# Alternating long and short head pairs in a transformer layer, and two weight scans moved to earlier pairs

## The chip, the cores and the metric

The kernel runs on one core of a Trainium2 chip. Its time is that of one execution on the device, in microseconds, taken as the median of several runs; less is better. TensorE (PE) does the matmuls, VectorE (DVE) and ScalarE (ACT) the elementwise work, GpSimd (POOL) some of it too, and SyncE (SP) issues most of the DMAs, the transposes among them. Each engine works through its own list of instructions in order and waits on semaphores for the others.

## The reference

One layer (DEPTH is 1) over 2048 positions of width 1024, in float32. The part that the change touches is the attention:

```python
h = rmsnorm(x, attn_norm_g[l])
proj = h @ w_in[l]
qa, ka, va, qb, kb, vb = jnp.split(proj, 6, axis=-1)
oa = chunked_band_attention(...)   # 8 heads, each query chunk of 64 sees 9 key chunks
ob = diff_attention(...)           # 4 heads of two maps each, every earlier key is seen
x = x + jnp.concatenate([oa, ob], axis=-1) @ w_out[l]
h = rmsnorm(x, ffn_norm_g[l])
u = causal_dwconv(h @ w_up[l], conv_w[l], conv_b[l])
gate, val = jnp.split(u, 2, axis=-1)
x = x + (jax.nn.silu(gate) * val) @ w_down[l]
```

The 8 band heads make four head pairs, numbered 0 to 3. The 4 differential heads, each of two maps, make four more, numbered 4 to 7.

## The kernel before

All products are made in float16 with each operand split into a high and a low part, three matmuls for one. First the normalised input is made and transposed (`make_h`), and the first pair's keys, values and some queries are projected. Then `attention()` goes through the eight head pairs in the order of the list `ORDER`, 16 row tiles of 128 queries each. Pairs 0 to 3 have **short rows**: a row tile sees at most 640 keys. Pairs 4 to 7 have **long rows**: row tile i sees (i + 1) x 128 keys, up to 2048, and the tiles are taken in the order 0, 15, 1, 14 and so on, so that a long tile follows a short one.

A step is one row tile. Its front (`front_a` for short rows, `front_b` for long ones) makes the scores on TensorE (L434), adds the bias and takes the maximum on VectorE into an `St` buffer (L478 and L537), takes the exponential on ScalarE (L486 and L544), splits the result into high and low halves (`phl`, on ScalarE, VectorE and GpSimd) and transposes it by DMA from SP (`pt<-phl`, L489 and L565). Its back (`back_a`, `back_b`) multiplies by the values (L509, L583), two steps later (`LAG`). Between the fronts and backs stand portions of projection work (`units`, L375): the remaining queries of this pair, and keys, values and first queries of the next one. A pair has 48 portions, the last but one 32 and the last 28 (`CHUNKS`). A portion is 6 matmuls of 512 columns for keys and values, or 12 of 256 columns for queries.

`beside(n)` lists what else is put into which step of the n-th pair (n counts from 0, by place in `ORDER`): the loading and scaling of the next pairs' weights (`scan_w`, `load_w`), and at the end three pieces of preparation for what comes after. `scan_wo` loads the eight row blocks of `w_out`, 512 KB each, through the two `wraw` buffers, and squares and sums each on ScalarE (L606) into `wam`. `scan_wd` loads two row blocks of `w_down` and takes their maxima on VectorE (L614, then `wd_factor`); its result is first used in the feed-forward stage. `load_wo` in the last pair uses `wam`, loads `w_out` a second time and makes its two halves. The output projection (`out_proj`) begins in the last pair's last steps; after it come the feed-forward stages.

The instructions' order on each engine is decided when the program is built: fronts and backs are issued with high priority, so a scheduler lets them pass the portions and the pieces of `beside`.

## Time and profile before

| | us |
|---|---|
| median of 3 runs | 2524.24 |
| lowest, highest | 2523.07, 2527.94 |
| the profiled execution's own time | 2528.28 |
| its span, first to last instruction | 2526.5 |
| attention, first pair's first factor to last pair's last | 81.0 to 1103.8 |
| mean granted TensorE clock | 0.975 |

| engine | busy us | share |
|---|---|---|
| TensorE (matmul) | 2379.4 | 94% |
| VectorE | 1846.0 | 73% |
| ScalarE | 1354.3 | 54% |
| GpSimd | 1164.6 | 46% |

The busy time of an engine is the union of its instructions. A matmul's end is modelled in the profile, and at a lower granted clock the same matmul counts as busy for longer. The granted clock is given as a share of 2.4 GHz: 1.00 is that, 0.50 is 1.2 GHz, and a value between them is a mean over the stretch.

### The profile page before, as it was taken

The page shows a single profiled execution, that of the slowest core. Times are in us where ns is not written, and L with a number is a line of the kernel's source. Part 1 is how long each engine was busy: PE and PEld are TensorE (multiplying, and loading weights), DVE is VectorE, ACT ScalarE, POOL GpSimd, SP SyncE. Part 2 cuts the span into 40 slices and gives each one's busy share as a digit, 9 for nine tenths or more (in the row PEclk, how much of TensorE's full clock was granted, in tenths as well). Part 3 has the DMA queues.
Part 4 walks back from the last instruction along what each step waited for, and adds up shares of the span by engine and source line. Part 5 has one row for each costly group of instructions (what it writes and reads, how often), then busy time and mean ns, then how long its engine had stood idle before and what let it go on. Part 6 is the DMA issues. An engine that isn't in the chain of part 4 may idle for free.

```text
span 2526.5 us, 42303 instructions
## 1 busy us (share of the span) xinstructions
PE 2379.4 (94%) x15382; PEld 1219.7 (48%) x15382; DVE 1846.0 (73%) x4359; ACT 1354.3 (54%) x2399; POOL 1164.6 (46%) x1127
## 2 busy tenths in 40 slices
PE   6999899999899988997978999999999999999998
PEld 5655555555565555543433444444444444444443
DVE  8678787568757885766566888888888776656555
ACT  7566566456655666644335666566556553333322
POOL 3343443234323332224234665666566464766654
PEclk9999899999999999998999999999999999999999
DMA  6154457635673579895995324333333339323322
GB/s 192 29 101 88 94 104 139 121 73 96 134 143 73 100 128 226 162 242 167 277 225 154 123 96 129 106 121 97 123 112 111 105 111 398 101 88 113 109 88 80
DMA packets 625378, 333.34 MB, mean 132 GB/s; under 512 B 447864, under 2 KB 592528, under 8 KB 623760
## 3 DMA queue, kind: packets, MB, share of 16 engines
q1 hardware_dynamic: 615264, 316.15, 50.2%
q0 software_dynamic: 2432, 8.42, 0.9%
q10 hardware_dynamic: 7472, 6.06, 0.8%
q8 instruction: 120, 1.97, 0.3%
q14 instruction: 90, 0.74, 0.1%
HBM read 145.73 MB, written 82.08 MB: 90 GB/s over the span
## 4 chain that ended last, share of the span: by engine, by line
PE 36%; DVE 6%; DMA 3%; ACT 3%; issue 2%; POOL 2%; SPq 1%; ACTq 0%; DVEq 0%; POOLq 0%
PE mm L859 21%; PE mm L1258 13%; DMA wd<-gd 2%; DVE Y L1058 1%; SPq L1093 1%; PE omm L654 1%; DVE wdhl L889 1%; ACT wuraw L959 1%; DMA T<-td 1%; DMA wdraw<-in_w_down_dram 0%; DMA wd<-wdd 0%; ACT Y L1062 0%; ACT wdhl L886 0%; DVE hl L681 0%; POOL wuhl L977 0%
## 5 line engine op out<-in xcount | busy, mean ns | idle before, releaser
L859 PE MATMUL mm<-T,wuhl 128*128 128x512 f16 x3696 | 809.0, 381 | 18.2 <-ACT tmp L1030 14.9
L859 PEld LDWEIGHTS <-wuhl 128*128 128x128 f16 x3696 | 363.4, 99 | 456.2 <-issue 25.5
L1258 PE MATMUL mm<-wd,ghl 128*128 128x512 f16 x1848 | 401.9, 380 | 4.7 <-ACT ghl L133 3.5
L375 PEld LDWEIGHTS <-whl 128*128 128x128 f16 x2976 | 273.1, 99 | 233.6 <-issue 81.4
L375 PE MATMUL mm<-h,whl 128*128 128x512 f16 x1440 | 349.2, 385 | 0.0
L434 PE MATMUL s<-ks,qs 64*128 64x256 f16 (+3 forms) x2160 | 282.1, 295 | 29.0 <-DVE mx L478 14.4
L1258 PEld LDWEIGHTS <-ghl 128*128 128x128 f16 x1848 | 180.7, 98 | 225.2 <-ACT ghl L133 4.8
L563 POOL TENSOR_TENSOR phl<-St,phl 128x1024 f16<-128x1024 f32 (+7 forms) x96 | 155.7, 1633 | 248.8 <-ACT phl L562 233.7
L1058 DVE SCALAR_TENSOR_TENSOR Y<-U,taps,Y 128x1024 f32<-128x1024 f32 x176 | 256.9, 1460 | 6.2 <-ACT Y L1054 4.6
L544 ACT ACTIVATE St<-St,nb,sc 128x1024 f32<-128x1024 f32 (+4 forms) x192 | 187.9, 979 | 50.3 <-DVE nb L541 50.3
L133 ACT ACTIVATE ghl<-wd,gsc 128x384 f16<-128x384 f32 (+1 forms) x176 | 106.6, 660 | 196.6 <-DMA wd<-gd 92.1
L134 DVE SCALAR_TENSOR_TENSOR ghl<-wd,gsc,ghl 128x384 f16<-128x384 f32 (+1 forms) x176 | 137.0, 812 | 94.3 <-ACT ghl L133 94.0
L375 PE MATMUL mq<-h,whl 128*128 128x256 f16 x1536 | 205.0, 278 | 0.0
L488 POOL TENSOR_TENSOR phl<-St,phl 128x640 f16<-128x640 f32 (+2 forms) x64 | 80.9, 1264 | 255.0 <-ACT phl L487 246.3
L434 PEld LDWEIGHTS <-qs 64*128 64x128 f16 x2160 | 114.4, 96 | 152.5 <-issue 108.0
L537 DVE CUSTOM_DVE_ANT_0 St<-s,near,mxb 128x512 f32<-128x512 f32 (+2 forms) x280 | 166.7, 620 | 25.5 <-PE s L434 19.8
L654 PE MATMUL omm<-wohl,oT 128*128 128x512 f16 x672 | 155.6, 386 | 18.5 <-DVE x L660 18.5
L889 DVE SCALAR_TENSOR_TENSOR wdhl<-wdraw,wd_sc,wdhl 128x128 f16<-128x128 f32 x132 | 141.5, 1087 | 30.8 <-ACT wdhl L886 29.7
L968 POOL TENSOR_TENSOR Sx<-wuraw 128x512 f32<-128x512 f32 x44 | 77.4, 1760 | 163.2 <-ACT wuraw L959 156.0
L1062 ACT ACTIVATE Y<-Y 128x1024 f32<-128x1024 f32 x44 | 46.5, 1057 | 182.2 <-DVE Y L1058 182.2
L486 ACT ACTIVATE St<-St,nb,sc 128x640 f32<-128x640 f32 (+4 forms) x128 | 107.9, 843 | 59.3 <-DVE nb L483 58.1
L562 ACT ACTIVATE phl<-St 128x1024 f16<-128x1024 f32 (+7 forms) x96 | 75.6, 802 | 114.1 <-DMA pt<-phl 56.6
(229 smaller groups left out, 3765.9 us busy)
## 6 DMA issues: line engine op xcount, KB each, us to landing
wd<-gd SPq DMA_DIRECT2D x88, 256.0 KB, 2.8
wuraw<-in_w_up_dram SPq DMA_DIRECT2D x42, 512.0 KB, 5.2
gd<-Y SPq DMA_DIRECT2D x42, 512.0 KB, 2.8
wdraw<-in_w_down_dram SPq DMA_DIRECT2D x154, 128.0 KB, 2.8
wd<-wdd SPq DMA_DIRECT2D x11, 1792.0 KB, 13.1
wdd<-wdhl SPq DMA_DIRECT2D x41, 448.0 KB, 2.7
wraw<-in_w_in_dram SPq DMA_DIRECT2D x24, 512.0 KB, 3.9
td<-hl SPq DMA_DIRECT2D x24, 512.0 KB, 5.0
```

What stands on the lines that cost most here:

```text
L134: V.scalar_tensor_tensor(lo, src, scale, hi, ALU.mult, ALU.subtract)
L375: nc.tensor.matmul(ps, lhsT=hl[:, a, c, :], rhs=h[:, b, c, t0:t1], start=n == 0, stop=n == 3 * NC - 1)
L434: nc.tensor.matmul(ps[hd], lhsT=qs[a:b, qa, qc], rhs=ks[a:b, ka, kc], start=n == 0, stop=n == 2)
L486: A.activation(St, St, AF.Exp, bias=nb[:, hd:hd + 1], scale=w["sc"], accum_out=l[:, hd:hd + 1])
L537: V.tensor_tensor_reduce(Sm[hd][g][:, a0:a0 + b - a], ps[hd][:, :b - a], bias, 1.0, m[hd], ALU.add, ALU.max, mx[:, hd, f:f + 1])
L544: A.activation(Sm[hd][g], Sm[hd][g], AF.Exp, bias=nb[:, hd:hd + 1], scale=w["sc"], accum_out=l[:, hd, g:g + 1])
L563: nc.gpsimd.tensor_tensor(hl[:, 1], Sm[0][g], hl[:, 0], ALU.subtract)
L654: nc.tensor.matmul(ps[n], lhsT=oc[:, a], rhs=wo[ORDER[c]][:, b, n * TG:(n + 1) * TG], start=k == 0, stop=k == 3 * NC - 1)
L859: nc.tensor.matmul(ps, lhsT=hl[:, a, wop, c * P:(c + 1) * P], rhs=Tt[:, b, c, :], start=start and k == 0, stop=k == 11, skip_group_check=n ...
L889: V.scalar_tensor_tensor(dst, src, scale, h, ALU.mult, ALU.subtract)
L1058: V.scalar_tensor_tensor(Y, self.U[j][:, tap:D + tap], self.u.taps[j][:, tap:tap + 1], Y, ALU.mult, ALU.add)
L1258: nc.tensor.matmul(ps[m].rearrange("p (c n) -> p c n", c=4), lhsT=g[kb][:, a, go], rhs=wd[kb][:, :, c_, wo_], start=kb == k0 and k == 0, s ...
```

## The change

The list `ORDER` is changed so that long and short rows alternate: 4, 0, 5, 1, 6, 2, 7, 3. The first and the last pair stay what they were. `scan_wo` moves from step 10 of the last but one pair to step 10 of the third pair, and `scan_wd` from step 13 of the last but one pair to step 10 of the fifth. The numbers of portions still go by place: the last but one pair, now the long pair 7, has 32.

```diff
-        ORDER = [4, 5, 0, 6, 1, 7, 2, 3]
+        ORDER = [4, 0, 5, 1, 6, 2, 7, 3]
...
-            if n == NH2 - 2:
+            if n == 2:
                 todo[10, 0] = scan_wo
-                todo[13, 0] = scan_wd
+            if n == 4:
+                todo[10, 0] = scan_wd
             if n == NH2 - 1:
                 todo[8, 1] = load_wo
```

The first place is SP's list at the passage from the first pair to the second. `pt<-phl` at L565 is the transpose of a long row tile's probabilities, at L489 of a short one's (the middle number of the shape is the count of 128 x 128 blocks), `ost<-ohl` and `oTd<-ost` carry the pair's output away. Before:

```order
L565 DMA_TRANSPOSE pt<-phl 128x2x128 x2
L447 DMA_TRANSPOSE ost<-ohl 128x8x128
L451 DMA oTd<-ost 256x1x512
L565 DMA_TRANSPOSE pt<-phl 128x16x128 x2
L447 DMA_TRANSPOSE ost<-ohl 128x8x128
L565 DMA_TRANSPOSE pt<-phl 128x4x128
```

Now:

```order
L565 DMA_TRANSPOSE pt<-phl 128x2x128
L489 DMA_TRANSPOSE pt<-phl 128x4x128
L447 DMA_TRANSPOSE ost<-ohl 128x8x128
L489 DMA_TRANSPOSE pt<-phl 128x8x128
L451 DMA oTd<-ost 256x1x512
L489 DMA_TRANSPOSE pt<-phl 128x12x128
L489 DMA_TRANSPOSE pt<-phl 128x16x128
```

The last long tile of the first pair was followed by the second pair's longest tile at once; now short tiles follow it.

The second place is ScalarE's list around the squares of `w_out` (L606, `woraw` is a row block). L486 and L544 are the exponentials of short and long rows, L487 and L562 the copies to the high half, L588 the squares of a long pair's output, L133 the high halves of projected keys, values and queries. Before, in the seventh pair:

```order
L486 ACTIVATE St,l<-St,nb,sc 128x640 x2
L606 ACTIVATE woraw,wam<-woraw 128x1024
L487 ACTIVATE phl<-St 128x640 x2
L606 ACTIVATE woraw,wam<-woraw 128x1024
L133 ACTIVATE qs<-mq 128x256
L486 ACTIVATE St,l<-St,nb,sc 128x640 x2
L606 ACTIVATE woraw,wam<-woraw 128x1024
```

Now, in the third pair:

```order
L606 ACTIVATE woraw,wam<-woraw 128x1024
L544 ACTIVATE St,lb<-St,nb,sc 128x1024
L544 ACTIVATE St,lb<-St,nb,sc 128x640
L544 ACTIVATE St,lb<-St,nb,sc 128x1024
L544 ACTIVATE St,lb<-St,nb,sc 128x640
L588 ACTIVATE o,ssq<-osb 128x128
L606 ACTIVATE woraw,wam<-woraw 128x1024
L544 ACTIVATE St,lb<-St,nb,sc 128x640 x2
```

Each square stood between the two exponentials of a short row; now it stands between those of long rows, four of them for a row of more than 1024 keys.

## Rows read from the trace of the kernel before

**Rows 1.** The page, busy time and share of the span of each engine.
```profile
PE 2379.4 (94%) x15382; PEld 1219.7 (48%) x15382; DVE 1846.0 (73%) x4359; ACT 1354.3 (54%) x2399; POOL 1164.6 (46%) x1127
```

**Rows 2.** Busy time by stretch (columns in the first row): the eight pairs.
```profile
core 0: us, PE busy (x) PEld busy (x) DVE busy (x) ACT busy (x) POOL busy (x), PEclk, DMA share, GB/s
81.00:231.40 150.40, 143.24 (x1182) 83.68 (x1180) 111.32 (x367) 88.34 (x177) 59.99 (x34) 0.98 0.43 83
231.40:382.20 150.80, 137.58 (x1101) 77.51 (x1099) 121.36 (x396) 91.58 (x193) 59.47 (x34) 0.94 0.50 93
382.20:497.50 115.30, 112.04 (x1063) 66.09 (x1062) 73.09 (x264) 65.19 (x136) 35.92 (x24) 0.97 0.73 134
497.50:644.90 147.40, 140.06 (x1090) 76.12 (x1088) 115.15 (x362) 85.95 (x176) 56.04 (x32) 0.96 0.49 89
644.90:756.40 111.50, 105.13 (x1066) 64.35 (x1064) 75.47 (x262) 66.03 (x138) 35.51 (x24) 0.97 0.70 137
756.40:900.00 143.60, 136.38 (x1095) 75.06 (x1094) 113.15 (x362) 87.22 (x178) 55.98 (x32) 1.00 0.48 90
900.00:999.10 99.10, 86.96 (x920) 54.34 (x919) 72.00 (x255) 64.71 (x139) 30.32 (x21) 0.95 0.92 181
999.10:1103.80 104.70, 95.25 (x982) 56.64 (x978) 72.99 (x219) 61.40 (x119) 20.94 (x17) 0.92 0.92 183
```

**Rows 3.** Waits of TensorE in the second pair: total us, times, longest us.
```profile
PE s L434 <- DVE mxb L537: 6.6, 7, 3.0
PE o L583 <- DMA pt<-phl: 5.7, 3, 3.3
```

**Rows 4.** Timeline of TensorE in the second pair: start us, us, what, [idle before].
```profile
261.81 1.43 PE L434 MATMUL s<-ks,qs 64*128 64x512 f16 x3 [3.02 <-DVE mxb L537]
```

**Rows 5.** Busy time by stretch: from that wait on.
```profile
258.80:272.00 13.20, 10.19 (x64) 6.63 (x65) 10.68 (x38) 4.86 (x10) 3.64 (x3) 0.61 0.61 117
```

**Rows 6.** The page, groups: projection matmuls; busy us, mean ns of one.
```profile
L375 PE MATMUL mm<-h,whl 128*128 128x512 f16 x1440 | 349.2, 385 | 0.0
```

**Rows 7.** Busy time by stretch, projections (L375) alone: fifth and seventh pair.
```profile
644.90:756.40 111.50, 70.43 (x383) 36.10 (x381) 0.97 0.70 137
...
900.00:999.10 99.10, 51.12 (x298) 26.99 (x296) 0.95 0.92 181
```

**Rows 8.** Busy time by stretch: sixth pair's quarters, then seventh's second, third, eighth's first.
```profile
756.40:791.50 35.10, 34.19 (x258) 17.96 (x257) 22.82 (x74) 18.61 (x38) 7.81 (x5) 1.00 0.37 67
791.50:826.30 34.80, 34.59 (x289) 19.49 (x287) 27.30 (x92) 20.94 (x45) 17.04 (x9) 1.00 0.45 91
826.30:871.50 45.20, 39.77 (x326) 22.05 (x324) 40.36 (x130) 27.76 (x58) 16.26 (x10) 1.00 0.55 101
871.50:900.00 28.50, 27.84 (x231) 15.56 (x229) 22.67 (x72) 19.90 (x40) 14.88 (x9) 1.00 0.55 102
...
918.90:939.70 20.80, 16.00 (x197) 10.45 (x197) 20.17 (x68) 15.51 (x30) 9.89 (x6) 1.00 0.80 146
939.70:978.60 38.90, 31.62 (x338) 19.40 (x337) 21.70 (x70) 22.73 (x43) 11.55 (x7) 0.91 1.05 215
...
999.10:1019.40 20.30, 16.96 (x189) 10.45 (x185) 12.49 (x53) 11.95 (x32) 4.57 (x5) 0.92 0.89 160
```

**Rows 9.** Line L606 (ns min/median/max), and ScalarE's wait in the seventh pair's third quarter.
```profile
L606 ACT ACTIVATE woraw<-woraw x8: 1040/1052/1058, 938.2 to 987.8; 128x1024 f32<-128x1024 f32 x8
L606 ACT ACTIVATION_READ_ACCUMULATOR woraw<-woraw x8: 185/186/191, 939.2 to 988.7; 128x1 f32 x8
...
ACT woraw L606 <- DMA woraw<-in_w_out_dram: 7.2, 4, 3.4
```

**Rows 10.** Line L614 and one small line of the factor behind it (ns min/median/max).
```profile
L614 DVE TENSOR_REDUCE wd_m<-wdfirst x2: 1220/1220/1220, 988.6 to 994.3; 128x1 f32<-128x1024 f32 x2
...
L110 DVE TENSOR_SCALAR pw<-wd_m x1: 150/150/150, 999.0 to 999.0; 128x1 f32<-128x1 f32 x1
```

## The prediction

> **What bounds the kernel now.** I read the page's busy shares first: TensorE (PE) is busy 94% of the span [rows 1]. Then I cut the attention stage into its eight head pairs. A cut is the moment at which the factor of a pair's first exponential is made on VectorE (L541 for a long pair, L483 for a short one): 81.0, 231.4, 382.2, 497.5, 644.9, 756.4, 900.0, 999.1 and 1103.8 us. The reader is to see in that table [rows 2] what the two kinds of pair look like. A long pair with a full ration of projections beside it takes 143.6 to 150.8 us with VectorE busy 74 to 80%. A short one takes 111.5 and 115.3 us with VectorE at 63 and 68%. The seventh pair, short and with 32 projection portions in place of 48, takes 99.1 us; it and the last pair are the only ones with the DMA engines at 0.92. TensorE is the bound in all of them: even in the second pair it is idle only 150.8 - 137.6 = 13.2 us. Its idle time is made of waits for VectorE's max passes and for the transposes of the probabilities [rows 3].
>
> So the work of TensorE is the same before and after, and the question is how much idle time each pair gets. Everything from 1103.8 us on (feed-forward and the rest) is the same program in the same order, and I leave it as it is.
>
> **Part 1: the order of the pairs.** Before, the kinds run L L S L S L S S; after, L S L S L S L S. The first (L) and last (S) stay. For pairs two to seven the rows give 150.8 + 115.3 + 147.4 + 111.5 + 143.6 + 99.1 = 767.7 us. After the change these six are three short pairs with 48 portions, each behind a long one, two long pairs with 48 portions, each behind a short one, and one long pair with 32 portions. The first two kinds are in the trace: short (115.3 + 111.5) / 2 = 113.4, long behind short (147.4 + 143.6) / 2 = 145.5 [rows 2]. That is 3 x 113.4 + 2 x 145.5 = 631.2 us. It contains one gain already: the only long pair behind a long one took 150.8 us, 5.3 more than the mean of the others. There TensorE waited 3.02 us for a max pass [rows 4], 27 us after the cut, and its granted clock over the next 13.2 us was 0.61 [rows 5].
>
> A long pair with 32 portions is in no row, and it decides the sign: it breaks even at 767.7 - 631.2 = 136.5 us. The 16 portions that go are projections of keys and values, 6 matmuls of 512 columns each, so 96 matmuls. One costs 349.2 / 1440 = 0.243 us [rows 6], together 23.3 us. If TensorE alone counted, the pair would take 145.5 - 23.3 = 122.2 us (lower end); if VectorE held it, nothing would go: 145.5 us (upper end). The short pair shows both at work: between a short pair with 48 portions and the one with 32 the trace counts 383 - 298 = 85 projection matmuls fewer [rows 7], 20.7 us, and the pair became 113.4 - 99.1 = 14.3 us shorter.
>
> I go by quarters of four steps, taken from the sixth pair, which ran at full clock [rows 8]. Each quarter loses 4 portions, 5.8 us of TensorE, but I let none be shorter than VectorE's work at a busy share of 0.89, which is what the third quarter has now (40.36 of 45.20). First: 35.1 - 5.8 = 29.3. Second: 34.8 - 5.8 = 29.0, but VectorE 27.30 / 0.89 = 30.7. Third: 40.36 / 0.89 = 45.3, so no gain: 45.2. Fourth: 28.5 - 5.8 = 22.7, but 22.67 / 0.89 = 25.5. Sum 130.7. The sixth pair is 1.9 us faster than the mean long pair: 132.6.
>
> Then the clock. In [rows 5] it stood at its lower level, 1.2 GHz, for 2 x 0.39 x 13.2 = 10.3 us after the wait of 3.02 us, and cost half of that, 5.1 us. I add half such a fall, 2.6: **135.2 us**, 1.3 below break-even. The Trainium skill, "TensorE: Matmul & The Clock Gate", Part 1, says that the slow state is the array's default and that activity releases it, so that a stall is paid a second time at half speed afterwards. The trace agrees at that wait, and does not at the third quarter of the sixth pair, where TensorE was idle 5.4 us in short pieces and the clock stayed at 1.00; by the rule taken strictly the pair would get a whole fall, 137.7 us, and the order alone would cost 1.2 us.
>
> **Part 2: the last pair.** It stays a short pair with 28 portions, but follows a long one with idle DMA engines instead of a short one with full ones. Its first quarter lost 20.30 - 16.96 = 3.3 us to waits, and its clock was 0.92 [rows 8], another 0.08 x 20.3 = 1.6 us: the most to win is 4.9. Against it, a short pair behind a long one brings the tail of the long rows' VectorE work. In the second quarter of the seventh pair, which also has few projections, VectorE was busy 20.17 of 20.80 us and TensorE idle 4.8. I take -3 (from -4.9 to +4.8), nearer to the first row since the transposes then have free DMA engines.
>
> **Part 3: the squares of w_out.** Eight loads of 512 KB and eight Square passes on ScalarE, 1052 + 186 ns each, 9.9 us [rows 9]. They leave the seventh pair (its cost there is inside the 99.1 us that part 1 subtracts) and go to step 10 of the third pair, in the third quarter of a long pair. There ScalarE is busy 27.76 of 45.20 us [rows 8]. With the squares it is 37.7, and it also waits in its queue for the loads, 7.2 us in the seventh pair. Behind a waiting square stand the exponentials of the next rows, and for those the max passes' St buffers. On SP the loads stand between transposes and wait for one of two buffers; the other wraw loads move behind them, still 3 steps ahead of use. Lower end 0 (ScalarE has room for all), upper end 9.9 + 7.2 = 17.1. I take 4, near the lower end, because the DMA engines are at 0.55 there and not at 1.05 [rows 8], so the loads should be there in time.
>
> **Part 4: the maxima of w_down.** Two passes of 1220 ns on VectorE [rows 10] and four or five small ones of about 150 ns, 3.2 us. In the seventh pair VectorE has room (21.70 of 38.90 us in its third quarter [rows 8]); in the fifth pair's third quarter VectorE is the busiest engine. From 0 to 3.2; I take 1.5. Nothing later waits for them: the first user is the feed-forward.
>
> **Sum.** 631.2 + 135.2 - 767.7 = -1.3; -3 for the last pair, +4, +1.5: **+1.2 us**. The profiled execution took 2528.3 us (its span 2526.5); it would be 2529.5. The three timed runs have their median 4 us lower, at 2524.2, so I forecast 2525 us: no change.
>
> **The rivals.** A, faster: VectorE is no floor at 0.89. In the second quarter of the seventh pair it reached 0.97 [rows 8]. With 0.97 the four quarters are 29.3, 29.0, 41.6 and 23.4, together 123.3 instead of 135.2, and without the fall of the clock the two other long pairs go as the sixth did, 2 x 1.9 less. That is 15.7 below my sum: 2510 us. For it: the one long pair without a fall, and that two long pairs in a row are gone. Against it: the third quarter has kept 0.89 in the fourth and sixth pairs.
>
> B, slower, by ScalarE in the third pair: busy 27.76 + 9.9 and waiting 7.2 fills 44.9 of 45.2 us, so ScalarE and no longer VectorE sets that quarter, and the max passes wait for their buffers. It decides as soon as squares and their waits together pass 40.4 - 27.8 = 12.6 us, VectorE's own load. Price 17.1 instead of 4: 2538 us. Against it: the loads come through emptier DMA engines.
>
> C, slower, by VectorE in the seventh pair: with fewer projections TensorE has nothing to do while it waits for max passes, and the 16 portions' time stays in the pair as idle time: 145.5 instead of 135.2, 2536 us. It decides when VectorE's share passes 0.89 over more than the third quarter. For it: VectorE's 113.15 us of 143.6 stay nearly whole while TensorE's 136.4 fall by 23.3 to 113.1, level with them.
>
> **Chances.** No change (my forecast) 0.36, A 0.34, C 0.17, B 0.13. What a measurement of this kernel can tell from no change is about 0.2%, 5 us. A's cases go to faster, B's and C's to slower, but each has a share within 5 us, and my own case spills to both sides: faster 0.36, same 0.33, slower 0.31. The range must reach A's 2510 and B's 2538 with a little beyond, because the falls of the clock will lie elsewhere after any reordering: by [rows 2] they cost 38 us now (one minus the clock, times the length, summed over the eight pairs). So 2508 to 2541. My own case alone would be 2519 to 2531.
>
> **What would show it.** In the new profile, cut at the same places: six pairs of 113, 145, 113, 145, 113 and 135 us. Step 1 is right if the short second pair takes about 113 us with less idle time than 13 us; the seventh pair's length decides between A (123), me (135) and C (145), with VectorE's share in its third quarter beside it. B shows as a third pair well above 150 us with ScalarE waiting for the w_out loads. The DMA share of the seventh pair should fall from 0.92 to about 0.5. I am wrong in kind if the time after 1103.8 us moves, or if the short pairs behind long ones come out longer than the two that the trace has.

## The result

The changed kernel is slower: 2544.16 us in the median of 4 executions (2538.01 to 2549.66), against 2523.65 us (2521.34 to 2527.94) for the kernel before beside it. The ratio is 1.0077, 95% interval 1.0059 to 1.0096, that is +20 us. The forecast was 2525 us, and its range ended at 2541: it missed. Of all executions behind this document one stands apart, of the run new_wo_moved, with 4812.62 us, and it is left out of that run's median and ratio.

### The profile page after: what moved, and what is told of

Read it like the earlier page. It is cut to its first block, busy times and chain, and to the rows that moved or that the text cites. A ratio compares the mean times of both kernels' runs of the same rounds, so it can differ in the third digit from the quotient of the medians.

```text
span 2541.7 us, 42331 instructions
## 1 busy us (share of the span) xinstructions
PE 2391.7 (94%) x15382; PEld 1225.3 (48%) x15382; DVE 1844.0 (73%) x4359; ACT 1357.1 (53%) x2399; POOL 1169.6 (46%) x1127
## 4 chain that ended last, share of the span: by engine, by line
PE 41%; DVE 3%; DMA 3%; SPq 2%; ACT 1%; issue 1%; POOL 1%; ACTq 0%; DVEq 0%; POOLq 0%
PE mm L860 28%; PE mm L1259 13%; SPq L1094 2%; DMA wd<-gd 2%; DMA T<-td 1%; DVE Y L1059 0%; DVE hl L681 0%; ACT wuraw L960 0%; PE omm L654 0%; DVE wdhl L890 0%; DVE T L674 0%; DMA x1k<-in_x_dram 0%; POOL wd L1236 0%; ACT xn L669 0%; POOL wd L1237 0%
## 5 line engine op out<-in xcount | busy, mean ns | idle before, releaser
L375 PEld LDWEIGHTS <-whl 128*128 128x128 f16 x2976 | 278.2, 101 | 235.9 <-issue 80.3
L375 PE MATMUL mm<-h,whl 128*128 128x512 f16 x1440 | 352.1, 388 | 0.0
L544 ACT ACTIVATE St<-St,nb,sc 128x1024 f32<-128x1024 f32 (+4 forms) x192 | 187.9, 980 | 45.7 <-DVE nb L541 45.5
L133 ACT ACTIVATE ghl<-wd,gsc 128x384 f16<-128x384 f32 (+1 forms) x176 | 106.6, 660 | 197.5 <-DMA wd<-gd 97.1
L375 PE MATMUL mq<-h,whl 128*128 128x256 f16 x1536 | 212.0, 284 | 0.0
L134 DVE SCALAR_TENSOR_TENSOR ghl<-wd,gsc,ghl 128x384 f16<-128x384 f32 (+1 forms) x176 | 135.7, 805 | 94.5 <-ACT ghl L133 93.8
L537 DVE CUSTOM_DVE_ANT_0 St<-s,near,mxb 128x512 f32<-128x512 f32 (+3 forms) x280 | 167.3, 622 | 25.1 <-PE s L434 22.4
L486 ACT ACTIVATE St<-St,nb,sc 128x640 f32<-128x640 f32 (+4 forms) x128 | 107.9, 844 | 54.1 <-DVE nb L483 51.4
L562 ACT ACTIVATE phl<-St 128x1024 f16<-128x1024 f32 (+7 forms) x96 | 75.5, 801 | 102.8 <-DMA pt<-phl 58.5
```

Source lines behind the costliest of these rows:

```text
L134: V.scalar_tensor_tensor(lo, src, scale, hi, ALU.mult, ALU.subtract)
L375: nc.tensor.matmul(ps, lhsT=hl[:, a, c, :], rhs=h[:, b, c, t0:t1], start=n == 0, stop=n == 3 * NC - 1)
L486: A.activation(St, St, AF.Exp, bias=nb[:, hd:hd + 1], scale=w["sc"], accum_out=l[:, hd:hd + 1])
L537: V.tensor_tensor_reduce(Sm[hd][g][:, a0:a0 + b - a], ps[hd][:, :b - a], bias, 1.0, m[hd], ALU.add, ALU.max, mx[:, hd, f:f + 1])
L544: A.activation(Sm[hd][g], Sm[hd][g], AF.Exp, bias=nb[:, hd:hd + 1], scale=w["sc"], accum_out=l[:, hd, g:g + 1])
```

## The profile after

The profiled execution took 2543.52 us (span 2541.7), 15.2 more than the one of before. First the busy line of the page, which answers to [rows 1].

```profile
PE 2391.7 (94%) x15382; PEld 1225.3 (48%) x15382; DVE 1844.0 (73%) x4359; ACT 1357.1 (53%) x2399; POOL 1169.6 (46%) x1127
```

The same number of instructions on every engine, and nearly the same busy time. Only TensorE is busy for 12 us more, with the same 15382 matmuls. Next the eight pairs, cut at the same places and with the same columns as [rows 2]; the sum of the answer stands below, then everything behind attention.

```profile
82.70:238.90 156.20, 149.12 (x1186) 87.49 (x1184) 112.88 (x371) 90.86 (x182) 60.60 (x34) 0.95 0.41 80
238.90:351.70 112.80, 105.16 (x1051) 63.82 (x1050) 76.81 (x261) 65.65 (x137) 36.00 (x24) 0.95 0.73 135
351.70:502.00 150.30, 140.65 (x1059) 74.07 (x1057) 112.22 (x358) 92.78 (x187) 58.14 (x32) 0.97 0.56 114
502.00:617.50 115.50, 107.55 (x1099) 66.86 (x1097) 77.54 (x264) 67.51 (x143) 35.90 (x24) 0.99 0.75 135
617.50:763.90 146.40, 138.59 (x1094) 76.03 (x1093) 116.49 (x367) 84.14 (x171) 56.92 (x32) 0.97 0.48 96
763.90:882.30 118.40, 108.21 (x1063) 65.51 (x1061) 75.97 (x263) 68.63 (x142) 35.55 (x24) 0.96 0.69 130
882.30:1015.10 132.80, 119.61 (x994) 68.17 (x993) 113.24 (x353) 76.62 (x160) 50.39 (x29) 0.95 0.47 91
1015.10:1119.30 104.20, 93.85 (x949) 54.84 (x948) 74.88 (x241) 65.17 (x130) 24.29 (x18) 0.93 0.89 176
sum 1036.60, PE 962.74 PEld 556.79 DVE 760.04 ACT 611.37 POOL 357.79; mean PE 120.34 PEld 69.60 DVE 95.01 ACT 76.42 POOL 44.72
...
1119.30:2541.70 1422.40, 1367.17 (x6329) 618.41 (x6327) 1016.19 (x1604) 693.79 (x1063) 784.78 (x885) 0.98 0.46 141
```

Behind attention 1422.4 us pass, before it was 2526.5 - 1103.8 = 1422.7: nothing is lost there. Attention took 1036.6 us in place of 1022.8. By the sums, TensorE was idle 1036.6 - 962.7 = 73.9 us; before, the eight rows of [rows 2] give 1022.8 - 956.6 = 66.2. The other 6.1 us are the same matmuls counting as busy for longer. Most of that is the lower clock (1.2 GHz): one minus the clock, times the length, makes 42 us over these eight rows, where the prediction counted 38 before.

One execution is not enough to say so. Both kernels were profiled a second time; here are the sums of attention and the sixth pair's row, first before again, then after again.

```profile
755.30:902.30 147.00, 140.99 (x1098) 77.35 (x1097) 113.05 (x360) 87.59 (x178) 56.02 (x32) 0.97 0.46 88
...
sum 1021.70, PE 958.57 PEld 554.24 DVE 754.85 ACT 610.27 POOL 353.42; mean PE 119.82 PEld 69.28 DVE 94.36 ACT 76.28 POOL 44.18
```

```profile
765.20:883.20 118.00, 108.49 (x1063) 65.56 (x1061) 75.89 (x263) 68.63 (x142) 35.53 (x24) 0.96 0.69 131
...
sum 1039.60, PE 963.79 PEld 556.88 DVE 758.08 ACT 611.36 POOL 357.86; mean PE 120.47 PEld 69.61 DVE 94.76 ACT 76.42 POOL 44.73
```

Idle 63.1 and 75.8 us now (I had expected before's 66 to repeat within 2). Over the two profiles of each kernel attention is longer by 15.9 us: 10.2 us more idle time and 5.7 us more busy time. The profiled executions as wholes differ by 17.8 us in the mean (2527.2 and 2544.9); the 1.9 us between lie behind attention, where two profiles of one kernel already differ by that much (1422.7 and 1420.2 before). To the medians' 20 us it is 2 more, since both profiled executions of before stand above its median.

Who makes TensorE wait: the longest groups in all of attention, first in the kernel before (total us, times, longest us), then after.

```profile
PE o L583 <- DMA pt<-phl: 15.8, 14, 3.3
PE s L434 <- DVE mx L478: 14.4, 14, 2.9
PE s L434 <- DVE mxb L537: 13.1, 13, 3.0
PE o L509 <- DMA pt<-phl: 11.0, 7, 4.0
```

```profile
PE s L434 <- DVE mxb L537: 25.0, 26, 2.9
PE s L434 <- DVE mx L478: 11.0, 16, 1.8
PE o L583 <- DMA pt<-phl: 8.9, 9, 2.2
PE o L509 <- DVE osb L513: 7.8, 6, 2.1
```

The transposes got better (26.8 to 13.8 us, the second row for L509 is 4.9), VectorE got worse: its max passes go from 27.5 to 36.0 us. There are more waits, and the longest is no longer than before. The second profiles agree: transposes 28.6 and then 15.2 us, max passes 26.3 and then 37.6.

## The experiments

The theories that the expectations name: **1**, the order alone makes the loss (1a: by a long pair with 32 portions in the seventh place, 1b: by short pairs behind long ones from the start); **2**, the two scans beside long rows make it; **3**, it belongs to any rearrangement, by waits that fall elsewhere and clock that falls with them; **4**, the squares of w_out in the third pair; **5**, the maxima of w_down on VectorE in the fifth; **6**, the parts do not add up, since the scheduler makes other lists for every engine each time; **7**, TensorE's waits for VectorE's max passes are the price of the order. All ratios are to the kernel before, run beside them on the same chip.

| run | median us | ratio [95%] | attention | TensorE busy | idle |
|---|---|---|---|---|---|
| before_again | 2525.46 | 1.0010 [0.9996, 1.0024] | 1021.7 | 958.6 | 63.1 |
| after_again | 2545.02 | 1.0085 [1.0057, 1.0113] | 1039.6 | 963.8 | 75.8 |
| order_only | 2533.85 | 1.0036 [1.0024, 1.0048] | 1033.6 | 961.9 | 71.7 |
| scans_only | 2548.17 | 1.0087 [1.0069, 1.0105] | 1042.1 | 975.9 | 66.2 |
| renamed | 2533.83 | 1.0036 [1.0020, 1.0053] | 1036.8 | 965.9 | 70.9 |
| tail_as_before | 2548.53 | 1.0091 [1.0075, 1.0107] | 1046.4 | 973.9 | 72.5 |
| old_no_scans | 2525.22 | 1.0000 [0.9987, 1.0013] | 1019.1 | 963.5 | 55.6 |
| new_no_scans | 2538.32 | 1.0049 [1.0033, 1.0065] | 1037.3 | 966.9 | 70.4 |
| new_wo_moved | 2539.11 | 1.0051 [1.0031, 1.0070] | 1037.9 | 962.2 | 75.7 |
| new_wd_moved | 2547.70 | 1.0083 [1.0064, 1.0102] | 1058.7 | 979.4 | 79.3 |
| old_pool_both | 2535.22 | 1.0036 [1.0019, 1.0054] | 1038.4 | 964.0 | 74.4 |
| order_pool_both | 2540.97 | 1.0070 [1.0044, 1.0096] | 1040.6 | 966.7 | 73.9 |
| after_pool_both | 2533.79 | 1.0033 [1.0013, 1.0053] | 1035.3 | 960.9 | 74.4 |
| old_step12 | 2528.55 | 1.0019 [1.0005, 1.0032] | 1026.7 | 962.9 | 63.8 |
| order_step12 | 2531.59 | 1.0031 [1.0018, 1.0045] | 1032.9 | 960.1 | 72.8 |
| old_o_free | 2548.53 | 1.0092 [1.0074, 1.0110] | 1050.9 | 971.0 | 79.9 |
| order_o_free | 2554.87 | 1.0114 [1.0092, 1.0137] | 1060.2 | 977.7 | 82.5 |
| after_o_free | 2542.78 | 1.0067 [1.0050, 1.0085] | 1039.6 | 966.0 | 73.6 |

The last three columns are the sums over attention of one profiled execution of each, which can lie off its run's median: by 12 us in new_wd_moved, by 4 to 7 us in seven others. No version beats the kernel before.

**order_only**, the new list with the scans where they were.

```diff
-        ORDER = [4, 5, 0, 6, 1, 7, 2, 3]
+        ORDER = [4, 0, 5, 1, 6, 2, 7, 3]
```

> The order of pairs alone is changed (4, 0, 5, 1, 6, 2, 7, 3); both scans stay in the last but one pair, which is now the long pair 7. Theory 1, the order makes the loss (more short waits of TensorE in the short pairs and in the seventh): 12 to 22 us slower than before, near 2540. Theory 2, the scans in long pairs make it: within 5 us of before, near 2525; the scans would then have to cost nothing beside pair 7. Theory 3, any rearrangement of the list costs some 5 to 15 us by where the falls of the clock come to lie: 5 to 15 us slower.

Measured +0.36%, 9 us: about half of the loss, below theory 1's 12 to 22 us and inside theory 3's 5 to 15. The third and fifth pair took 152.1 and 148.7 us, without any scan in them, where I had put 145.5. **scans_only**, the kernel before with the scans moved, there beside short rows:

```diff
-            if n == NH2 - 2:
+            if n == 2:
                 todo[10, 0] = scan_wo
-                todo[13, 0] = scan_wd
+            if n == 4:
+                todo[10, 0] = scan_wd
```

> The order of pairs is that of before; the squares of w_out go to step 10 of the third pair (here the short pair 0) and the maxima of w_down to step 10 of the fifth (short pair 1). Theory 1: within 5 us of before, since the order is untouched, or up to 5 us faster because the seventh pair loses its 7.2 us of waiting for the loads. Theory 2: 5 to 15 us slower. Theory 3: 5 to 15 us slower, since the scheduler's lists move too.

Measured +0.87%, 22 us, as much as the whole change, and above all that the three theories had allowed (15 us). The third and fifth pair of this run, then what ScalarE waited for in the one and VectorE in the other:

```profile
386.70:507.10 120.40, 113.27 (x1022) 66.46 (x1021) 73.14 (x261) 71.79 (x147) 35.92 (x24) 0.93 0.76 158
...
657.70:773.50 115.80, 110.85 (x1050) 66.15 (x1050) 77.86 (x269) 65.43 (x137) 34.92 (x24) 0.97 0.73 141
```

```profile
ACT woraw L606 <- DMA woraw<-in_w_out_dram: 11.3, 6, 3.7
```

```profile
DVE wd_m L614 <- DMA wdfirst<-in_w_down_dram: 6.1, 2, 5.0
```

Beside short rows, with the DMA engines at 0.73 to 0.76, each scan holds its engine while it waits for its load, and the pairs grow by 5.1 and 4.3 us over [rows 2]. The third does so with 41 matmuls fewer (1022 for 1063); the fourth has 55 more (1145 for 1090) and takes 3.2 us longer, so work of the third moved behind the cut. From the third to the sixth pair the growth is 16.6 us, the first two and the last add 2.0 and 5.3, and the seventh, which lost the scans, became 4.6 us shorter (94.5). How much of the loss is the waits for late loads can't be read off pair by pair.

**renamed**: the kinds in the old order, other pairs in it. **tail_as_before**: alternating at the start, then two long and two short.

```diff
-        ORDER = [4, 5, 0, 6, 1, 7, 2, 3]
+        ORDER = [4, 7, 1, 5, 2, 6, 0, 3]
```

> The kinds stand as before (long, long, short, long, short, long, short, short), only which pair of a kind stands where is changed (4, 7, 1, 5, 2, 6, 0, 3); scans as before. Same shapes and same counts everywhere. Theories 1 and 2: within 3 us of before. Theory 3, that any other list would be slower because the one of before is a lucky one: 5 to 15 us slower.

Measured +0.36%, but the control is spoilt. The lists of all engines are row for row those of before up to 1081 us. Behind that they differ, since the output projection multiplies the blocks of w_out in `ORDER`'s order, and the last pair took 112.7 us in place of 104.7, with 9.1 us of waits for transposes in place of 4.2. So this run doesn't test other lists in the first seven pairs. They took 924.1 us against 918.1 all the same, in an execution 5.8 us above its run's median, and the sixth 148.0 where before had 143.6.

```diff
-        ORDER = [4, 5, 0, 6, 1, 7, 2, 3]
+        ORDER = [4, 0, 5, 1, 6, 7, 2, 3]
```

> Alternation at the start, the end as before: long, short, long, short, long, long, short, short (4, 0, 5, 1, 6, 7, 2, 3), scans as before in the short seventh pair. Theory 1a, what costs is the long pair in the seventh place with 32 portions: within 5 us of before. Theory 1b, what costs is short pairs following long ones in the first places (first pair 156 and not 150 us, short pairs 115 to 118 and not 111 to 115): 8 to 15 us slower. Theory 2: within 5 us of before.

Measured +0.91%, 23 us: with a short seventh pair as before, the loss is as large as ever (and above the 8 to 15 of 1b). So 1a falls; a long pair with 32 portions is not needed for it, and by the same run neither are scans beside long rows (theory 2).

Then the two scans one by one, in the new order:

```diff
-            if n == NH2 - 2:
+            if n == 2:
                 todo[10, 0] = scan_wo
+            if n == NH2 - 2:
                 todo[13, 0] = scan_wd
```

> New order of pairs, the squares of w_out moved to the third pair as in the change, the maxima of w_down left in the seventh. The order alone gave +8 us, the change as a whole +20. Theory 4, the squares in the third pair (ScalarE waiting for their loads with exponentials behind them) make the difference: +17 to +22 us over before. Theory 5, the maxima on VectorE in the fifth pair make it: +6 to +11 us. Theory 6, neither in itself, but the lists that the scheduler makes: anything from +5 to +20, and the two moves do not add up.

```diff
             if n == NH2 - 2:
                 todo[10, 0] = scan_wo
-                todo[13, 0] = scan_wd
+            if n == 4:
+                todo[10, 0] = scan_wd
```

> New order of pairs, the maxima of w_down moved to the fifth pair as in the change, the squares of w_out left in the seventh. Theory 4: +6 to +11 us over before, like the order alone. Theory 5: +17 to +22 us. Theory 6: anything from +5 to +20.

Moving w_out's squares alone makes +0.51%, moving w_down's maxima alone +0.83%, as much as both together. Theory 4 had 17 to 22 us for the first and 6 to 11 for the second; measured are 13 and 21, and it falls.

Theory 5's 17 to 22 us for the second were met, but not where it put them: the fifth pair, with the maxima, took 146.4 and 146.3 us in the changed kernel's two profiles (151.7 in new_wd_moved's, 12 us above its run's median), and 148.7 and 145.8 in order_only and order_step12 without them. The sixth is longer: 118.4, 118.0 and 120.2 us in the three profiles of the new order with the maxima in the fifth pair, and 112.9, 112.0, 112.1 and 116.7 in the four without (order_only, order_step12, new_wo_moved, new_no_scans). In those three, and in none of the four, TensorE waits 3.16 us in it for VectorE. In the changed kernel ScalarE had waited for a transpose, VectorE for ScalarE, and TensorE for VectorE (start, length, what, idle before; the last line has the columns of [rows 2]):

```profile
827.39 1.36 ACT L487 ACTIVATE phl<-St 128x640 f16<-128x640 f32 x2 [4.07 <-DMA pt<-phl]
828.85 1.44 DVE L488 TENSOR_TENSOR phl<-St,phl 128x640 f16<-128x640 f32 x1 [5.13 <-ACT phl L487]
831.54 2.08 PE L355 MATMUL turned<-rows,turn 128*128 128x512 f32 x2 [3.16 <-DVE ks L134]
...
817.00:840.00 23.00, 17.87 (x178) 11.84 (x175) 9.34 (x30) 10.98 (x20) 6.81 (x4) 0.78 0.73 137
```

TensorE is idle for 5.1 of these 23 us, at a mean clock of 0.78; the rest of the pair ran at 1.00. Why the maxima, one pair earlier, bring that wait is not shown.

**old_no_scans** and **new_no_scans** leave both scans out and put constants in the place of their results:

```diff
-            for c in range(NC):
-                raw = wpool.tile([P, D], F32, name="woraw", tag="wraw", bufs=2)
...
+            V.memset(wam, 1.0)
...
+            V.memset(m, 0.08)
```

> Order of before, both scans left out: no loads, no squares, no maxima; wam and the first maxima are constants instead, so the scales of w_out and of the first part of w_down are not those of the data. What the scans cost where they were: theory 4 says some 5 to 10 us of the seventh pair (7.2 us of waiting for loads, idle 7.3 us in its third quarter), so 5 to 10 us faster than before; if they were free there, within 4 us.

> New order, both scans left out in the same way. If the order itself costs what the order-only run showed, 8 us more than the old order without scans. If the order only costs because the scans meet a long pair in the seventh place, the same as the old order without scans, within 4 us. Theory 4 for the change as made: it is 12 to 18 us below the change.

Without them the old order takes the same time as with them (1.0000): where they stood they cost nothing that the time shows. The new order costs 13 us without any scan, so the order has a price of its own. TensorE's waits for the max passes, old order first:

```profile
PE s L434 <- DVE mxb L537: 14.0, 11, 2.7
PE s L434 <- DVE mx L478: 12.4, 11, 2.7
```

```profile
PE s L434 <- DVE mx L478: 17.4, 17, 2.4
PE s L434 <- DVE mxb L537: 15.5, 14, 2.9
```

They go from 26.4 to 32.9 us. Theory 7 was formed on this, and three runs took work from VectorE: in short pairs GpSimd makes the low half of both heads.

```diff
-AP = (0,)
+AP = (0, 1)
```

> Order and scans of before; in short pairs GpSimd makes the low half of the probabilities for both heads and not for one (AP is (0, 1)), which takes 64 passes of 1061 ns, 68 us, off VectorE and gives GpSimd 64 passes of 1264 ns. Theory 7, TensorE's waits for VectorE's max passes make the loss of the new order: here the short pairs gain a little, 0 to 8 us faster than before. If later transposes weigh more (GpSimd is slower by 0.2 us a pass and has two in a row): up to 10 us slower.

> The same relief of VectorE in the new order, scans in the seventh pair. Theory 7: with VectorE relieved in the four short pairs the waits for max passes there go (17.6 us in the order-only run), so the distance to the old order with the same relief shrinks from 8 to 13 us to 0 to 5 us. Theory 6, the scheduler's list as such: the distance stays anywhere between 5 and 20 us.

> The change as made with the same relief. Theory 7: from 20 us slower than before to 5 to 12 us slower, 0 to 8 slower than the old order with the relief. Theory 6: stays 15 to 25 us slower than before.

In the old order this makes it 10 us slower; its third and fourth pair:

```profile
384.60:494.10 109.50, 104.06 (x1017) 62.31 (x1015) 65.62 (x247) 63.60 (x132) 52.80 (x39) 0.97 0.71 131
494.10:650.70 156.60, 147.02 (x1135) 81.23 (x1134) 118.80 (x361) 90.01 (x183) 58.38 (x34) 0.92 0.49 91
```

The short pair became shorter (115.3 to 109.5), but with 46 matmuls fewer in it, and the long one behind it, with 45 more, went from 147.4 to 156.6: most of what the one lost moved across the cut, and the two together take 3.4 us more. Theory 7 had a gain here; up to 10 us of loss stood beside it, for the case that later transposes weigh more. With this edit the whole change costs nothing more (2533.79 against 2535.22), as theory 7 had it and against the 15 to 25 us over before that theory 6 had. Yet the order alone costs 6 us: moving the scans now *gains* 7, though the two intervals just overlap. So neither theory's numbers hold in all three runs; that one move costs in one place and gains in another is what theory 6 says in general.

**old_step12** and **order_step12** start the squares of w_out two steps later:

```diff
-                todo[10, 0] = scan_wo
+                todo[12, 0] = scan_wo
```

> Order of before, squares of w_out still in the seventh pair, at step 12 and not 10: the lists differ only from there on. Theory 6, the list as such: 3 to 10 us slower than before in some place of the last two pairs. Otherwise, since leaving the scans out changed nothing: within 4 us of before.

> New order, squares in the seventh pair at step 12. If the loss of the order is in the kinds of passage between pairs and not in the scans: 8 to 15 us slower than before, like the order alone and like the new order without scans. Theory 6: anything from 0 to 22 us.

Old order +5 us, but not where theory 6 had put it. The lists are before's up to 975 us, in the seventh pair. The last two pairs took 204.0 us, before's two profiles 203.8 and 201.8; the first six, with before's own lists, 822.7 against 819.0 and 819.9. In the new order the scheduler makes the same five lists as for order_only, row for row, so this is order_only measured again: +9 and +8 us, in 21 executions. The first pair in the two, order_only first:

```profile
83.30:237.50 154.20, 146.71 (x1187) 85.89 (x1185) 112.14 (x371) 90.66 (x182) 60.63 (x34) 0.97 0.44 81
```

```profile
80.90:238.40 157.50, 149.48 (x1187) 87.79 (x1185) 113.03 (x373) 90.73 (x182) 60.65 (x34) 0.95 0.42 79
```

The same instructions in the same order, 3.3 us apart. That is how far one pair of one execution can be read. Even so, leaving the last three runs aside, the first pair took 154.2 to 157.5 us in all ten profiles whose second pair is short, and 150.1 to 152.9 in all seven whose second pair is long. In the changed kernel the trace shows how. ScalarE's timeline near 190 us (start, length, what, idle before), then TensorE's, then the stretch behind it (columns as in [rows 2]):

```profile
192.67 0.84 ACT L562 ACTIVATE phl<-St 128x768 f16<-128x768 f32 x1 [4.34 <-DMA pt<-phl]
193.42 0.61 ACT L442 ACTIVATE ohl<-osb 128x512 f16<-128x512 f32 x1
193.94 0.26 ACT L588 ACTIVATE o<-osb 128x128 f32<-128x128 f32 x1
```

```profile
194.38 2.19 PE L583 MATMUL o<-vs,pt 128*128 128x128 f16 x19 [2.03 <-ACT o L588]
```

```profile
194.10:204.30 10.20, 9.92 (x61) 6.22 (x60) 5.64 (x16) 5.32 (x14) 1.13 (x1) 0.50 0.57 117
```

ScalarE waits for a transpose to leave its buffer, a square that frees the PSUM bank `o` stands behind it, TensorE waits 2.03 us for that bank and then runs 10.2 us at 1.2 GHz, which costs it half, 5.1 us. In the kernel before the same L562 waited 3.4 us, and TensorE waited 0.71 us for the square, with no fall of the clock behind it.

The other profiles bear this out in part. In all ten TensorE waits 1.8 to 2.1 us for that square, 111 to 114 us behind the cut, and in the seven 0.6 to 0.9. A fall follows in eight of the ten and in none of the seven. The two of the ten without it, order_only and new_wd_moved, have the shortest first pairs, 154.2 and 155.1 us, but still longer than any of the seven, so the fall is not the whole price. New_wd_moved behind its wait of 2.05 us:

```profile
193.00:206.00 13.00, 10.95 (x110) 7.35 (x108) 9.74 (x28) 6.86 (x17) 1.64 (x1) 1.00 0.66 115
```

The last three runs take this wait away: the square writes into a scratch tile, so the bank is free when VectorE has read it.

```diff
-            A.activation(o, osb[:, t], AF.Square, accum_out=ssq[:, t:t + 1])
+            sq = sb.tile([P, P], F16, name="sq", bufs=1)
+            A.activation(sq, osb[:, t], AF.Square, accum_out=ssq[:, t:t + 1])
```

> The kernel before, with the squares of a long pair's output (L588) written to a scratch tile in SBUF and not back into the PSUM bank o, so that the bank is free as soon as VectorE has read it and TensorE's next back no longer waits for ScalarE. In the kernel before TensorE waits 1.9 us in all for L588, in 4 short waits, none over 0.8. Theory 7 (TensorE's waits and the falls of the clock behind them are the price of the order): -1 to -3 us here, 2521 to 2524, first pair 150 us as before. Theory 6 (any other list of instructions out of the scheduler moves the time by ten us or so, whatever it was meant for): anywhere from 2515 to 2545, and the waits that grow are not those for L588.

> The new order alone, the squares of w_out and the maxima of w_down where they were, and L588 into the scratch tile. Theory 7: the first pair loses its 5 to 6 us in the new order because TensorE waits 2 us for ScalarE's L588, which stands behind an L562 that waits for a transpose, and then runs 10 us at the lower clock; with the bank freed by VectorE that wait and that fall go, the first pair comes back from 154-157 to 151 us, and the time from 2533 to 2527, with the short pairs behind long ones still 113 to 116. Theory 6: the first pair may shorten or not, and the sum over the pairs moves by more than that in either direction.

> The changed kernel with L588 into the scratch tile. Theory 7: TensorE's 5.8 us of waits for L588 go (4 waits, longest 2.5), and the fall in the first pair with them: first pair 151 in place of 156, time 2534 to 2537 in place of 2544 or 2545. Theory 6: not additive, 2520 to 2550, and the distance to the kernel before with the same edit is not the 20 us of the unedited two.

Measured +0.92%, +1.14% and +0.67%: theory 7's forecast fails in all three, by some 26, 28 and 7 us; the first also passes theory 6's 2545. The first pair of old_o_free, then that of after_o_free, then two of TensorE's waits in old_o_free:

```profile
81.30:240.70 159.40, 151.94 (x1189) 86.98 (x1187) 117.40 (x367) 89.97 (x182) 60.10 (x34) 0.94 0.44 80
```

```profile
82.90:236.60 153.70, 146.17 (x1189) 85.00 (x1186) 117.78 (x369) 89.08 (x180) 60.43 (x34) 0.98 0.43 82
```

```profile
PE s L434 <- DVE mx L478: 24.9, 20, 4.8
PE s L434 <- DVE mxb L537: 21.1, 21, 3.8
```

In the old order the first pair grew by 9 us, in the changed kernel it lost 2.5. In order_o_free it took 160.7, and the wait for the bank stayed, 1.8 us, now for VectorE's reading of it (L587).

The waits for L588 are gone, and in old_o_free those for the max passes rose from 27.5 to 46.0 us, in an order of pairs that had not changed. The lists of all engines changed with the edit, and one thing that came of it can be read. VectorE's small factor L541 takes 0.29 us in the median of 64, but each that takes over 0.5 us has a GpSimd pass running beside it: 13 in the kernel before, 15.7 us together, and 27 in old_o_free, 35.4 us. One of these (the row of GpSimd joins two passes):

```profile
634.61 2.24 DVE L541 TENSOR_SCALAR nb<-mxb,nsc,lnk 128x2 f32<-128x2 f32 x1
634.69 3.00 POOL L563 TENSOR_TENSOR phl<-St,phl 128x1024 f16<-128x1024 f32 x2 [11.77 <-ACT phl L562]
```

ScalarE's exponentials waited for L541 50.3 us in before and 75.1 in old_o_free. The changed kernel has 14 such, 18.3 us, so this bears on these edits more than on the change, and no run tests it.

**What the runs show together.** The price of moving the scans is +22 us in the old order, +11 in the new one, -7 with the GpSimd edit (its intervals just overlap) and -12 with the scratch tile (1.0114 [1.0092, 1.0137] against 1.0067 [1.0050, 1.0085]). The price of the order is +9 with the scans late, +13 without them, +6 with either other edit (there the intervals overlap), and none with the scans early (2544 against 2548). So the move of the scans has no price of its own that could be added to the order's.

Two places of the loss are found. The first pair is some 5 us longer when the second is short, in every run but the last three. The sixth is some 5 us longer with the maxima in the fifth, though not together with the GpSimd edit (105.7 us, 108.6 without the move) or the scratch tile (114.1 and 115.1). For the rest theories 3 and 6 are what is left, by exclusion and not by a run that tests them alone. Of 15 distinct programs besides before and after that ran, old_no_scans and old_step12 stayed within 5 us, 13 were 8 to 30 us slower, and none was faster. But most of them change order or work together with the lists, renamed keeps before's lists nearly throughout, and old_no_scans has other lists and costs nothing. That any other list costs is therefore not shown, and neither is which property of before's lists makes them good, or whether they are just the best of several that were once tried.

## Why the prediction was wrong, point by point

**The step that failed is part 1's price list**: "short (115.3 + 111.5) / 2 = 113.4, long behind short (147.4 + 143.6) / 2 = 145.5". It took the length of a kind of pair in one execution of one set of lists as a constant of that kind, and left the first pair as it was. Against the forecast lengths of the eight (their sum, with the parts put in their pairs, 1024.0) the profile has 1036.6. By place: first +5.8, second -0.6, third +0.8, fourth +2.1, fifth -0.6, sixth +5.0, seventh -2.4, eighth +2.5; the first cut lies 1.7 us later. So two pairs make most of it. The first I had left at its 150.4; the runs show TensorE's wait for the square there, 2.0 us in place of 0.7, with a fall of the clock behind it. The sixth is one of the three "short behind long" pairs; the runs show the wait of 3.16 us there once the maxima stand in the fifth, so part 4's term was put in the wrong pair too. A third error hides behind part 3: without the squares the third pair took 152.1 and 151.9 us, not 145.5. The order alone was forecast by parts 1 and 2 at 1018.5 us for the eight pairs; order_only and order_step12 have 1033.6 and 1032.9, with the last pair at 106.8 and 106.6 in place of 101.7. The 143.6 that went into the price of the long pairs was one execution's luck: the same program took 147.0 there the second time, with 6.0 us idle and not 7.2, and a clock of 0.97 and not 1.00, and renamed and old_step12, with the same list there, took 148.0.

**The bound.** Right: TensorE stays the bound everywhere, and the question was its idle time. Wrong was to count idle time by kinds of pair. It rose by 7.7 us between the two first profiles while the waits for transposes fell by 13: the max passes' rose by 8.5, those for the backs' VectorE step (L513) from 1.8 to 7.8, those for the square (L588) from 1.9 to 5.8, and the rest came in small pieces.

**The seventh pair** was the step that I held to decide the sign. It came out right: 132.8 us (132.3 in the second profile) against 135.2, so neither A's 123 nor C's 145. Its quarters, with the columns of [rows 8]:

```profile
882.30:912.00 29.70, 29.70 (x222) 15.50 (x222) 24.18 (x83) 17.21 (x36) 9.04 (x5) 1.00 0.40 74
912.00:943.10 31.10, 23.89 (x225) 13.79 (x225) 28.00 (x91) 19.72 (x40) 18.91 (x10) 0.92 0.48 100
943.10:989.80 46.70, 42.95 (x344) 24.21 (x341) 39.65 (x118) 26.13 (x56) 13.67 (x9) 0.91 0.55 106
989.80:1015.10 25.30, 23.07 (x209) 14.67 (x209) 21.43 (x66) 13.57 (x31) 8.77 (x6) 1.00 0.41 75
```

Forecast 29.3, 30.7, 45.2 and 25.5 at full clock, measured 29.7, 31.1, 46.7 and 25.3. VectorE's share was 0.90 in the second quarter and 0.85 in the third: the floor of 0.89 held, roughly. The DMA share fell to 0.47, forecast 0.5. The clock's part was larger than the half fall that I put: 0.95 over 132.8 us, 6.6 us by one minus the clock. Less idle time made that good: 13.2 us, where 132.6 less TensorE's 113.1 left 19.5 in the forecast. So the length came out right partly by luck, and in new_wd_moved the same pair took 142.9. The right answer to the question that I held to decide was worth 2 us; the sign was decided elsewhere.

**Part 2, the last pair.** -3 was forecast, 104.2 us against 104.7 measured. Its first quarter still had 2.6 us of idle time where before had 3.3, and the fourth lost 2.8 where before lost nothing. The waits for transposes were gone from the pair, as I had meant; in the first quarter one of 2.5 us for the square of a long row came in their place.

**Part 3, the squares of w_out.** Forecast +4 in the third pair, with B at +17. The third pair took 150.3 us, 4.8 more than 145.5, as if the term were right; but order_only and order_step12 have 152.1 and 151.9 there without the squares, so the base was too low there and the squares added nothing that can be seen: the term came out right by luck. What they met, ScalarE's wait in the third pair:

```profile
ACT woraw L606 <- DMA woraw<-in_w_out_dram: 6.4, 2, 3.4
```

6.4 us, nearly the 7.2 of [rows 9]: the emptier DMA engines did not bring the loads much sooner. ScalarE had the room all the same, and B is refuted at its place.

**Part 4, the maxima.** Forecast +1.5 in the fifth pair. VectorE waited there for the load as follows, and the pair was no longer than forecast (146.4 against 147.0). What the move cost showed in the sixth.

```profile
DVE wd_m L614 <- DMA wdfirst<-in_w_down_dram: 1.7, 1, 1.7
```

**What would show it.** Two signs were named for an error in kind. The time behind attention did not move. The short pairs behind long ones did come out longer, 112.8, 115.5 and 118.4 us, mean 115.6 against 113.4 (114.5, 116.3 and 118.0 the second time). "The falls of the clock will lie elsewhere after any reordering" stood in the prediction too, as a reason for a little more range; it should have been a rival with a price of its own.

**The chances.** 31% stood on slower, but for B and C, neither of which happened. That the first pair, or the pair behind a moved scan, would grow was not among them.

## What to carry to other kernels

Where a scheduler writes the instruction lists, an edit's price need not be the sum of its parts: measure the edit in two surroundings before a cause is named; here one and the same move cost 22 us and gained 12. A control that should change nothing must be compared list by list first, or it may be testing less than it seems, as renamed did. Lengths of stages taken from one profile carry the luck of that execution, some 3 us on a pair of 150, so a forecast that rests on differences of 2 us between stages needs a second profile of the same program. And price the neighbours of a moved stage too: the first pair, with the same rows as before but another pair's projections beside it, took some 5 us more, and the sixth some 5 us more once the maxima stood in the fifth.

## What the runs showed of the hardware that was not expected

A fall of TensorE's clock can be dearer than the wait ahead of it: 2.03 us of waiting, then 10.2 us at a granted clock of 0.50, which is 1.2 GHz. The Trainium skill, "TensorE: Matmul & The Clock Gate", Part 1, has the slow state as the default and activity as what releases it, and this stretch agrees. The same wait does not always bring one: in new_wd_moved it took 2.05 us, and the stretch from 193 to 206 us has 1.00. Where the falls lie differs between executions of one program: the sixth pair of the kernel before had none in one profile (1.00) and a mean of 0.97 in the other, with less idle time in the second (6.0 us for 7.2).

More idle time did not go with longer waits: the changed kernel's longest wait for a max pass is 2.9 us against 3.0, but there are 42 of them in place of 27.

An engine that works its list in order passes a late load on to others: 512 KB loads that came late held ScalarE for 11.3 us in six waits in scans_only, and in the changed kernel a late transpose's buffer reached TensorE through a square of 0.26 us that stood behind it.

A small instruction of VectorE can be stretched beside a GpSimd pass: L541, on 128x2 elements, took between 0.28 and 2.24 us in old_o_free, and in the traces of before, after, old_o_free and order_o_free every one over 0.5 us had such a pass beside it.
